# First modulation on TensorE, zero fills left out, first attention's stores from GpSimd, stick-breaking in float32 with sigmoids in PSUM

## The chip, the cores and the metric

The kernel runs on one core of a Trainium2 chip. The metric is the device time of one execution in microseconds (us). The kernel before takes 4246.98 us, the median of 3 runs (4244.62 to 4251.69).

## What is computed

Two blocks, one after the other, on 1024 tokens of width 1024, float32 throughout. The parts that the change touches:

```python
# first block: modulation of layer 0, for the tokens and for 256 context tokens
shift, scale, gate = split(silu(c) @ ada_w[0] + ada_b[0], 3)
shift_c, scale_c, gate_c = split(silu(c_ctx) @ ada_w[0] + ada_b[0], 3)
# layer 0: attention (8 heads over 2 kv heads, 8 heads over a latent), out = (o * silu(gate)) @ w_out
# layer 1: Hyena; its filters h = (hid @ w3 + b3) * decay are carried into the frequency domain
# second block, layer 0: causal convolution beside stick-breaking attention (8 heads of 64)
z = q @ k.T / 8;  log_1m = where(causal, log_sigmoid(-z), 0)
between = reverse_cumsum(log_1m) - log_1m
wts = where(causal, exp(log_sigmoid(z) + between), 0);  o = wts @ v
# layer 1: gated linear recurrence; after both layers a mixture of 16 experts
```

## The kernel before, in words

One program of 45506 instructions on five engines; a scheduler orders the instructions of each engine's queue by the dependences of tiles, so that loads may stand ahead of where the source has them. A queue is served strictly in its order. Matrix products are made from float32 operands split into a high and a low part of type float32r (`split`, L100 on ScalarE and L104 on VectorE), three matmuls each (`mm3`, L108 to L110).

**Spectra of the Hyena filters.** `hy_spectra` and `_filters` (L921 to L1070) make the filters in 8 chunks: `prepare` loads w3 and b3, splits them into `wa` and `wb` (rows 64 and 96 of `wb` carry the bias's high and low part, rows 65 to 95 are filled with zeros, L1005), four steps of matmuls with `wa` and `wb` (L1038, L1039) give PSUM tiles that VectorE multiplies by the decay (`fb`, L1041) and splits (`sd`). `_spectrum` turns a chunk into frequencies with 8 calls of `base`, 18 matmuls each at most; after three of every four calls it takes one step of the work in `self.aside`, and one step of `_filters` after each call.

**The first modulation** is that work aside: `mods` (L222) loads 16 row blocks of `ada_wT` (512 KB each, SP queue, ring of 3). Even blocks are multiplied and summed on VectorE, once for c and once for c_ctx (L236); odd ones are multiplied on GpSimd (L233) and summed on ScalarE (L234). silu(c) and silu(c_ctx) are made on rows of 1024 on all 128 partitions. It must be done before chunk 3.

**First attention.** `_a_project` (L338) projects the 1280 tokens; each result is normalised, rotated, split, and kept in DRAM by `store` (the high part's DMA from the ScalarE queue, the low part's from the GpSimd queue, L421), by `vstore` (L426) and by `gate` (L477), both from the ScalarE queue: 38 high parts, 38 low parts, 20 values, 16 gates. A loop over 38 projections takes one step of `beside` (22 products for latent keys and values, then 12 for latent queries) after each from the tenth on, the rest behind the loop. The keys' table `S["k"]` has 160 rows a head: high part, low part, a row of ones (L428), 31 rows of zeros that two SP DMAs write (L432). `a_load` reads the tables back for `_a_attend`, from the GpSimd queue.

**Stick-breaking attention.** `ev_attend` (L1565) goes over 32 units (head, group of 256 queries). Each has two rows of 128 queries: `scores` (L1608, L1611) gives z in PSUM (ring of 2 tiles of two banks), ScalarE writes sigmoid(-z) to SBUF (`e`, ring of 4), VectorE scans it backwards (L1620, with an operand of zeros from one column), GpSimd subtracts neighbours (`w`, L1624). `turn` transposes the weights on TensorE (L1636) and splits them into `th` and `tl`; `gather` (L1650) multiplies both by the values, which `values` (L1506 to L1508) has stored as high and low part side by side; the two halves of the sum are added by L1654 and L1656.

## Time and profile before

| | us |
|---|---|
| median of 3 runs | 4246.98 |
| the profiled execution, its own time | 4247.26 |
| its span, from the first to the last instruction | 4245.5 |
| PE busy / VectorE (DVE) busy / ScalarE (ACT) busy / GpSimd (POOL) busy | 3659.2 / 2932.2 / 1777.8 / 1031.8 |
| mean granted clock of TensorE | 0.931 of full speed |

A stage is read with the table by stretches: busy time of each engine, the granted clock of TensorE, and what the DMA engines moved. Which wait holds a stage is read from the timeline, where the brackets give the idle time ahead of an instruction and what ended it. PE is TensorE, and PEld its weight loads; SPq and ACTq are the DMA issues of the SP and ScalarE queues.

### The profile page before, as it was taken

Reading aid. Unit: us, or ns where it says so; the run is one execution under the profiler, and the core shown is the slowest. Engines: PE = TensorE matmul, PEld = TensorE weight load, DVE = VectorE, ACT = ScalarE, POOL = GpSimd, SP = SyncE. Lnnn points to the kernel's source line nnn. Section 1 sums busy time; section 2 is a strip of 40 time slices with the busy share of each in tenths; the row PEclk is TensorE's granted clock in tenths of the full one; section 3 lists DMA queues with packets and bytes.
Section 4 is the critical chain, followed back from the end, with each engine's and each line's share of the span. In section 5 each row is a group of like instructions: output and inputs, shape, how many; then the busy total and the mean of one; then the engine's idle time right before and its main releaser. Section 6 shows DMA issues by size and latency. Waiting matters only on the chain. (4 is left out here: it accounts for less than half of the span.)

```text
span 4245.5 us, 45506 instructions
## 1 busy us (share of the span) xinstructions
PE 3659.2 (86%) x16880; PEld 2817.5 (66%) x16880; DVE 2932.2 (69%) x3280; ACT 1777.8 (42%) x2458; POOL 1031.8 (24%) x628
## 2 busy tenths in 40 slices
PE   5799779999989999686989957879999788889997
PEld 4787564445568777675757746667887576667885
DVE  7996427787656774999667869565665777556664
ACT  4554334344343211111443345535655544546663
POOL 4740011111010012786000034321112134311112
PEclk9899898999999999887999979989999899989998
DMA  4553364534146882433322241347777310368786
GB/s 159 167 177 92 109 173 125 157 85 119 35 144 230 280 282 70 147 131 126 137 73 77 69 110 43 136 152 272 288 292 256 136 45 31 109 228 307 288 295 210
DMA packets 224278, 675.20 MB, mean 159 GB/s; under 512 B 54775, under 2 KB 79915, under 8 KB 188980
## 3 DMA queue, kind: packets, MB, share of 16 engines
q1 hardware_dynamic: 144806, 521.72, 35.4%
q0 software_dynamic: 61200, 107.01, 9.1%
q10 hardware_dynamic: 18046, 43.52, 2.9%
q8 instruction: 134, 2.20, 0.2%
q14 instruction: 92, 0.75, 0.1%
HBM read 538.04 MB, written 133.94 MB: 158 GB/s over the span
## 5 line engine op out<-in xcount | busy, mean ns | idle before, releaser
L104 DVE TENSOR_TENSOR wl<-wraw,wh 128x1024 fp32r<-128x1024 f32 (+1 forms) x214 | 332.1, 1561 | 266.8 <-ACT wh L100 253.4
L100 ACT CAST wh<-wraw 128x1024 fp32r<-128x1024 f32 (+1 forms) x214 | 277.4, 1308 | 487.9 <-PE pj L109 164.8
L108 PE MATMUL pj<-hh,wh 128*128 128x512 f32 x1024 | 408.2, 399 | 24.3 <-DVE u L1164 12.2
L110 PE MATMUL pj<-hh,wl 128*128 128x512 f32 x1024 | 403.1, 394 | 1.5 <-DVE wl L104 1.5
L109 PE MATMUL pj<-hl,wh 128*128 128x512 f32 x1024 | 403.9, 395 | 0.0
L108 PE MATMUL mm<-hh,wh 128*128 128x512 f32 (+3 forms) x832 | 338.0, 407 | 37.6 <-ACT wh L100 19.4
L110 PE MATMUL mm<-hh,wl 128*128 128x512 f32 (+3 forms) x832 | 329.5, 397 | 7.7 <-DVE wl L104 7.7
L109 PE MATMUL mm<-hl,wh 128*128 128x512 f32 (+3 forms) x832 | 331.6, 399 | 1.0 <-POOL hl L104 0.8
L123 ACT ACTIVATE pt<-st 128x512 f32<-128x512 f32 x320 | 181.7, 599 | 221.0 <-PE st L678 211.2
L108 PEld LDWEIGHTS pj<-hh,wh 128*128 128x128 f32 x1024 | 194.9, 190 | 74.8 <-issue 18.4
L661 DVE TENSOR_REDUCE mx<-s 128x1 f32<-128x1280 f32 x124 | 184.5, 1488 | 82.2 <-PE s L658 81.2
L110 PEld LDWEIGHTS pj<-hh,wl 128*128 128x128 f32 x1024 | 194.4, 190 | 44.4 <-DVE wl L104 2.3
L109 PEld LDWEIGHTS pj<-hl,wh 128*128 128x128 f32 x1024 | 194.6, 190 | 43.9 <-issue 3.4
L236 DVE SCALAR_TENSOR_TENSOR modw<-modw,c 128x1024 f32<-128x1024 f32 x128 | 160.6, 1268 | 83.3 <-DMA modw<-in_mod_wT_dram 60.4
L108 PEld LDWEIGHTS mm<-hh,wh 128*128 128x128 f32 (+1 forms) x832 | 160.1, 193 | 86.0 <-issue 18.1
L104 DVE TENSOR_TENSOR l<-raw,h 128x1024 fp32r<-128x1024 f32 x128 | 165.2, 1322 | 66.0 <-ACT h L100 64.3
L684 PE MATMUL ps_o<-pt,v 128*64 128x512 f32 x640 | 209.8, 615 | 0.7 <-ACT pt L123 0.4
L1321 PE MATMUL py<-c_g,ph 128*128 128x256 f32 x512 | 135.8, 426 | 79.7 <-DVE ph L1200 79.7
L110 PEld LDWEIGHTS mm<-hh,wl 128*128 128x128 f32 (+1 forms) x832 | 159.6, 192 | 46.4 <-DVE wl L104 10.2
L109 PEld LDWEIGHTS mm<-hl,wh 128*128 128x128 f32 (+1 forms) x832 | 160.1, 192 | 39.5 <-DVE hl L877 1.9
L2199 POOL DMA_INDIRECT xg<-m_h,idx x50 | 62.4, 1247 | 467.8 <-PE xt L2113 421.2
L1321 PEld LDWEIGHTS py<-c_g,ph 128*128 128x128 f32 x512 | 107.4, 215 | 102.5 <-issue 67.2
(602 smaller groups left out, 9840.8 us busy)
## 6 DMA issues: line engine op xcount, KB each, us to landing
wraw<-in_ex_w_dram SPq DMA_DIRECT2D x128, 1024.0 KB
raw<-in_ex_w_dram SPq DMA_DIRECT2D x64, 1024.0 KB
modw<-in_mod_wT_dram SPq DMA_DIRECT2D x96, 512.0 KB
modw<-in_ada_wT_dram SPq DMA_DIRECT2D x48, 512.0 KB
m_y<-ys ACTq DMA_DIRECT2D x48, 512.0 KB
ks<-kt SPq DMA_DIRECT2D x64, 256.0 KB
wraw<-in_w_hy_in_dram SPq DMA_DIRECT2D x16, 1024.0 KB
kk<-ks SPq DMA_DIRECT2D x28, 512.0 KB
```

Of the source, the lines that this page charges most:

```text
L100: nc.scalar.copy(hi, src)
L104: e.tensor_tensor(out=lo, in0=src, in1=hi.bitcast(F32), op=ALU.subtract)
L108: nc.tensor.matmul(ps, wh, xh, start=first, stop=False)
L109: nc.tensor.matmul(ps, wh, xl, start=False, stop=False)
L110: nc.tensor.matmul(ps, wl, xh, start=False, stop=last)
L123: ins = act.activation(out, in_, func, **kw).ins
L236: nc.vector.scalar_tensor_tensor(out=junk, in0=w, scalar=1.0, in1=c, op0=ALU.mult, op1=ALU.mult, accum_out=o[:, j:j + 1])
L661: nc.vector.tensor_reduce(out=mx[:, j:j + 1], in_=s[:, :TK] if own else m3, op=ALU.max, axis=AX.X, negate=True)
L684: nc.tensor.matmul(ps_o[e * 64:(e + 1) * 64], st[2 * hp + e]["v"][:, kb], pt[:, e], start=kb == 0, stop=kb == NK - 1)
L1321: nc.tensor.matmul(py[:, j], d["ph"][:, r, cs], g[:, m, r], start=k == 0, stop=k == 3)
L2199: self.nc.gpsimd.indirect_dma_start(out=out, out_offset=None, in_=src, in_offset=bass.IndirectOffsetOnAxis(ap=ix, axis=0))
```

## The change

The first modulation becomes `first_mods`: the untransposed weights (8 loads of 1 MB, SP queue, ring of 2) are the moving operand of 32 float32 matmuls, 4 to a load, each with 32 columns (of which two carry silu(c) and silu(c_ctx)) and its own 32 output partitions; a copy, four transposes and two copies bring the result into columns. The spectra's PSUM ring gives up one of six banks for it. The bias rows of the filters are split once for all chunks and put into `wb` by two GpSimd DMAs a chunk, its zero rows are filled once. `S["k"]` loses its 31 zero rows, and what is read of it is 65 rows in place of 96. All stores of the first attention's projections are issued by GpSimd, and `beside` begins four projections later. The stick-breaking attention keeps the values and the weights whole in float32, works on both heads of a pair at once (64 output partitions each), takes rows in another order, and writes the sigmoid over z in PSUM, from where VectorE scans it.

```diff
...
+    def first_mods(self, pool, pp, outs):
...
+        nc = self.nc
+        sc = pool.tile([P, 8, 32], F32, name="mc")
+        nc.vector.memset(sc, 0.0)
+        self.act(sc[:, :, 0:2], self.vec("cond", 0, 16).rearrange("p (k c) -> p k c", c=2), AF.Silu)
+        yield
+        ps = pp.tile([P, 512], F32, name="md", tag="md")
+        ws = []
+        for k in range(9):
+            if k < 8:
+                w = pool.tile([P, 2048], F32, name="modw", tag="modw", bufs=2)
+                nc.sync.dma_start(w, self.a["ada_w0"][k * P:(k + 1) * P])
+                ws.append(w)
+            if k:
+                for q in range(4):
+                    nc.tensor.matmul(ps[32 * q:32 * q + 32], sc[:, k - 1], ws[k - 1][:, q * 512:(q + 1) * 512],
+                                     start=k == 1, stop=k == 8)
+            yield
+        t = pool.tile([P, 512], F32, name="mt")
+        nc.scalar.copy(t, ps)
+        yield
+        pt = pp.tile([P, 4, P], F32, name="md", tag="md")
+        for b in range(4):
+            nc.tensor.transpose(pt[:, b], t[:, b * P:(b + 1) * P], self.ident)
+        yield
+        for i, o in enumerate(outs):
+            nc.vector.tensor_copy(o[:, 0:16].rearrange("p (q b) -> p b q", b=4), pt[:, :, i::32])
+        yield
...
-            for name, shape in (("q", [8, 2, 64, T]), ("k", [2, 160, TK]), ("v", [P, 10, P]),
+            for name, shape in (("q", [8, 2, 64, T]), ("k", [2, 129, TK]), ("v", [P, 10, P]),
...
-                    (nc.gpsimd if i else nc.scalar).dma_start(ap_of(dst, i * off * pitch + t0, dims), src.bitcast(F32))
+                    nc.gpsimd.dma_start(ap_of(dst, i * off * pitch + t0, dims), src.bitcast(F32))
...
-                nc.scalar.dma_start(dst[:, b], t)
-            nc.sync.dma_start(ap_of(S["k"], 128 * TK, [[P, 10], [160 * TK, 2], [1, P]]),
+                nc.gpsimd.dma_start(dst[:, b], t)
+            nc.sync.dma_start(ap_of(S["k"], 128 * TK, [[P, 10], [129 * TK, 2], [1, P]]),
                               ap_of(self.ones1, 0, [[self.ones1.ap[0][0], 10], [0, 2], [1, P]]))
-            zero = self.blk64[0:31, 64:128]
-            for i in range(2):
-                nc.sync.dma_start(S["k"][i, 129:160].rearrange("r (b t) -> r b t", t=64),
-                                  ap_of(zero, 0, [zero.ap[0], [0, TK // 64], [1, 64]]))
...
-                nc.scalar.dma_start(S["gate"][m, :, pt[0]:pt[0] + 512], g)
+                nc.gpsimd.dma_start(S["gate"][m, :, pt[0]:pt[0] + 512], g)
...
-                if n >= 10:
+                if n >= 14:
...
-                kb = kp.tile([96, 1, TK], F32R, name="kb", tag="kb")
+                kb = kp.tile([65, 1, TK], F32R, name="kb", tag="kb")
...
-            nc.gpsimd.dma_start(qb[:, :, :n], qs[0:96, :, :n])
+            nc.gpsimd.dma_start(qb[0:64, :, :n], qs[0:64, :, :n])
...
-        with tc.tile_pool(name="sp_c", bufs=1) as cp, tc.tile_pool(name="sp_ps", bufs=6, space=PSUM) as pp, \
+        with tc.tile_pool(name="sp_c", bufs=1) as cp, tc.tile_pool(name="sp_ps", bufs=5, space=PSUM) as pp, \
...
+        b3 = wp.tile([8, 2, 256], F32, name="b3", tag="w3", bufs=1)
+        for o in range(2):
+            nc.sync.dma_start(b3[4 * o:4 * o + 4], ap_of(a["hy_b3"], 2 * o * D, [[256, 4], [D, 2], [1, 256]]))
+        bs = wp.tile([8, 2, 256], F32, name="bs", bufs=1)
+        bh, bl = [wp.tile([8, 2, 256], F32R, name="b" + q, bufs=1) for q in "hl"]
+        for d, op in ((0, ALU.add), (1, ALU.subtract)):
+            nc.vector.tensor_tensor(out=bs[:, d], in0=b3[:, 0], in1=b3[:, 1], op=op)
+        self.split(bh, bl, bs)
+        wbs = [wp.tile([97, 2, 256], F32R, name=f"wb{i}", bufs=1) for i in range(2)]
+        for t in wbs:
+            nc.vector.tensor_copy(t[64:96].rearrange("p a b -> p (a b)"), self.zero_row(512)[64:96])
...
-            b3 = wp.tile([97, 2, 256], F32, name="b3", tag="b3", bufs=1)
             nc.sync.dma_start(w3, a["hy_w3"].rearrange("k (o d c) -> k o d c", o=2, d=2)[:, o, :, cs])
-            nc.sync.dma_start(b3[64:97], ap_of(a["hy_b3"], o * 2 * D + ch * 256, [[0, 33], [D, 2], [1, 256]]))
...
                 nc.gpsimd.tensor_tensor(out=ws[:, d], in0=w3[:, 0], in1=w3[:, 1], op=op)
-                nc.gpsimd.tensor_tensor(out=bs[64:97, d], in0=b3[64:97, 0], in1=b3[64:97, 1], op=op)
             wa = wp.tile([P, 2, 256], F32R, name="wa", tag="wa", bufs=2)
-            wb = wp.tile([97, 2, 256], F32R, name="wb", tag="wb", bufs=2)
-            b3h = wp.tile([97, 2, 256], F32R, name="b3h", tag="b3h", bufs=1)[96:97]
+            wb = wbs[(o * 4 + ch) % 2]
             nc.scalar.copy(wa, ws)
             nc.vector.tensor_tensor(out=wb[0:64], in0=ws[0:64], in1=wa[0:64].bitcast(F32), op=ALU.subtract)
-            nc.vector.tensor_copy(wb[64:96].rearrange("p a b -> p (a b)"), self.zero_row(512)[64:96])
-            nc.scalar.copy(wb[64:65], bs[64:65])
-            nc.scalar.copy(b3h, bs[96:97])
-            nc.vector.tensor_tensor(out=wb[96:97], in0=bs[96:97], in1=b3h.bitcast(F32), op=ALU.subtract)
+            for r, t in ((64, bh), (96, bl)):
+                nc.gpsimd.dma_start(wb[r:r + 1], t[o * 4 + ch:o * 4 + ch + 1])
...
-                t = tp.tile([P, 4, 2, 64], F32R, name="vhl", tag="vhl")
-                src = ps.rearrange("p (h e) -> p h e", e=64)
-                nc.scalar.copy(t[:, :, 0], src)
-                nc.vector.tensor_tensor(out=t[:, :, 1], in0=src, in1=t[:, :, 0].bitcast(F32), op=ALU.subtract)
-                nc.sync.dma_start(S["ev"][4 * c:4 * c + 4, :, b, :].rearrange("h p e -> p h e"),
-                                  t.rearrange("p h a e -> p h (a e)").bitcast(F32))
+                t = tp.tile([P, 256], F32, name="vs", tag="vhl")
+                nc.scalar.copy(t, ps)
+                nc.sync.dma_start(S["ev"][:, b, c * 256:(c + 1) * 256], t)
...
+                q, k = [ip.tile([P, 2, 2 * T if n == "k" else T], F32R, name=n, tag=n) for n in "qk"]
+                v = ip.tile([P, 8, P], F32, name="v", tag="v")
...
-                nc.gpsimd.dma_start(v, S["ev"][2 * hp:2 * hp + 2].rearrange("h p b e -> p h (b e)"))
+                nc.gpsimd.dma_start(v, S["ev"][:, :, hp * P:(hp + 1) * P])
...
-                e = wp.tile([P, T], F32, name="e", tag="e", bufs=4)[:, :n]
-                self.act(e, z[:, :n], AF.Sigmoid, scale=-1.0)
+                e = z[:, :n]
+                self.act(e, e, AF.Sigmoid, scale=-1.0)
...
-                w = wp.tile([P, T], F32, name="w", tag="w", bufs=6)[:, :n]
+                w = wp.tile([P, T], F32, name="w", tag="w", bufs=8)[:, :n]
...
-                th = wp.tile([P, 2, 256], F32R, name="th", tag="th", bufs=5)
-                tl = wp.tile([P, 2, 256], F32R, name="tl", tag="tl", bufs=5)
+                t = wp.tile([P, 2, 256], F32, name="wt", tag="wt", bufs=8)
...
-                    self.split(th[:, 0], tl[:, 0], pt[:, 0].rearrange("p j q -> p (j q)"))
-                    self.split(th[:, 1, P:], tl[:, 1, P:], pt[:, 1, 1])
...
                 else:
-                    self.split(th, tl, pt.rearrange("p b j q -> p b (j q)"))
...
+                    nc.scalar.copy(t, pt.rearrange("p b j q -> p b (j q)"))
+                return t
+            def gather(hp, g, ps_o, c, ts):
+                last = c == g
                 for b in range(2):
                     q0 = P if last and b == 1 else 0
-                    for x, t in enumerate((th, tl)):
-                        nc.tensor.matmul(ps_o[:, q0:], st[h]["v"][:, c + b], t[:, b, q0:],
-                                         start=c == 0 and b == 0 and x == 0, stop=last and b == 1 and x == 1)
+                    for e in range(2):
+                        nc.tensor.matmul(ps_o[e * 64:e * 64 + 64, q0:], st[2 * hp + e]["v"][:, 2 * c + b],
+                                         ts[e][:, b, q0:], start=c == 0 and b == 0, stop=last and b == 1)
                 if last:
-                    tmp = wp.tile([P, 256], F32, name="tmpo", tag="tmpo")
-                    nc.scalar.copy(tmp[64:128], ps_o[64:128])
-                    r = h % 2 * 64
-                    nc.vector.tensor_tensor(out=o[r:r + 64, 4 + h // 2, g * 256:(g + 1) * 256], in0=tmp[64:128],
-                                            in1=ps_o[0:64], op=ALU.add)
+                    nc.scalar.copy(o[:, 4 + hp, g * 256:(g + 1) * 256], ps_o)
...
-            todo = [(2 * hp + e, 3 - i if e == 0 else i) for hp in range(4) for i in range(4) for e in range(2)]
+            todo = [(hp, g) for hp in range(4) for g in (3, 0, 2, 1)]
+            rows = [(2 * hp + e, 2 * g + j) for hp, g in todo for j in range(2) for e in range(2)]
             es, ws, pend = {}, {}, []
-            for i in range(-2, len(todo)):
-                if i >= 0 and i % 8 == 2 and i < 24:
-                    load(i // 8 + 1)
-                if i >= 0:
-                    h, g = todo[i]
+            for r in range(-6, 4 * len(todo)):
+                i, t = r // 4, r % 4
+                if i >= 0 and i % 4 == 0 and t == 3 and i < 12:
+                    load(i // 4 + 1)
+                if 0 <= r + 4 < len(rows):
+                    ws[r + 4] = weights(*es.pop(r + 4))
+                if r + 6 < len(rows):
+                    es[r + 6] = scores(*rows[r + 6])
+                if i < 0:
+                    continue
+                hp, g = todo[i]
+                if t == 0:
                     ps_o = pp.tile([P, 256], F32, name="po", tag="po")
-                for t in range(4):
-                    if t < 2 and 0 <= i + 1 < len(todo):
-                        ws.setdefault(i + 1, []).append(weights(*es[i + 1][t]))
-                    if t < 2 and i + 2 < len(todo):
-                        q = todo[i + 2]
-                        es.setdefault(i + 2, []).append(scores(q[0], 2 * q[1] + t))
-                    if i >= 0 and t <= g:
-                        pend.append((h, g, ps_o) + turn(ws[i], 2 * g + 2, 2 * t))
-                    if len(pend) > 2:
-                        gather(*pend.pop(0))
+                if t <= g:
+                    pend.append((hp, g, ps_o, t, [turn([ws[4 * i + e], ws[4 * i + 2 + e]], 2 * g + 2, 2 * t)
+                                                  for e in range(2)]))
+                if len(pend) > 2:
+                    gather(*pend.pop(0))
...
-            self.aside = self.mods(mp, a["ada_wT"][0], ("c", "c_ctx"), (m["l0"], m["c0"]), 0, 16, 3, 2)
+            mpp = tc.alloc_tile_pool(name="mod_ps", bufs=1, space=PSUM)
+            self.aside = self.first_mods(mp, mpp, (m["l0"], m["c0"]))
+            self.step()
...
```

## Rows read from the trace of the kernel before

**Rows 1.** Table by stretches: stretch, us, busy and instructions by engine, granted clock, DMA share, GB/s.

```profile
52.00:304.00 252.00, 206.02 (x1468) 197.39 (x1468) 238.86 (x337) 138.38 (x252) 151.91 (x105) 0.91 0.47 154
208.00:220.00 12.00, 12.00 (x99) 11.83 (x98) 10.31 (x19) 7.36 (x15) 5.02 (x5) 1.00 0.42 142
415.00:525.00 110.00, 83.86 (x306) 61.70 (x305) 44.73 (x68) 41.55 (x58) 11.61 (x15) 0.84 0.38 108
525.00:606.00 81.00, 81.00 (x360) 61.47 (x359) 27.98 (x43) 28.63 (x46) 7.38 (x10) 1.00 0.61 164
2466.00:2663.00 197.00, 139.13 (x864) 122.86 (x864) 172.94 (x215) 101.17 (x215) 89.24 (x74) 0.88 0.24 60
```

**Rows 2.** Timeline, 13 to 53 us: start, us, instruction, [idle before, what ended it].

```profile
13.54 17.58 SPq L432 DMA_DIRECT2D s_k<-blk  x2
...
30.38 0.58 PE L1039 MATMUL pf<-wb,hb 97*128 97x256 f32 x1 [1.26 <-DVE wb L1008]
...
46.61 2.34 POOL L233 TENSOR_TENSOR modj<-modw,c 128x1024 f32<-128x1024 f32 x1 [28.57 <-DMA modw<-in_ada_wT_dram]
...
50.17 2.29 DVE L236 SCALAR_TENSOR_TENSOR modj<-modw,c 128x1024 f32<-128x1024 f32 x1 [19.84 <-ACT modj L234]
...
52.39 1.28 DVE L1041 TENSOR_TENSOR fb<-pf,dec 128x512 f32<-128x512 f32 x2
```

**Rows 3.** VectorE's groups, 50 to 304 us: count, busy us, mean ns, idle before.

```profile
L104 DVE TENSOR_TENSOR sd<-fb,sd 128x512 fp32r<-128x512 f32 x64 | 63.0, 1003 | 3.0 <-ACT sd L100 2.9
L1041 DVE TENSOR_TENSOR fb<-pf,dec 128x512 f32<-128x512 f32 x64 | 41.2, 676 | 0.0
L236 DVE SCALAR_TENSOR_TENSOR modw<-modw,c_ctx 128x1024 f32<-128x1024 f32 x7 | 21.7, 3096 | 0.0
...
L236 DVE SCALAR_TENSOR_TENSOR modj<-modw,c 128x1024 f32<-128x1024 f32 x7 | 9.6, 1365 | 19.8 <-ACT modj L234 19.8
...
L1008 DVE TENSOR_TENSOR wb<-bs,b3h 1x512 fp32r<-1x512 f32 x7 | 8.1, 1153 | 0.2
...
L1005 DVE CAST wb<-zero_col 32x512 fp32r<-32x512 f32 x6 | 5.5, 916 | 0.1
```

**Rows 4.** Stores of line 421, 397 to 570 us: ns min/median/max, first and last start.

```profile
L421 ACTq DMA_DIRECT2D s_km<-sth x15: 325/2179/9411, 397.8 to 568.2; - x15
L421 POOL DMA_DIRECT2D s_km<-stl x15: 586/796/798, 398.8 to 570.0; - x15
```

**Rows 5.** Waits, 415 to 525 us: who waited for whom, us, times, longest.

```profile
PE mm L297 <- ACT sqa L287: 21.4, 4, 7.0
```

**Rows 6.** Timeline from the end of the projections to the first scores.

```profile
617.80 11.90 ACTq L421 DMA_DIRECT2D s_qm<-sth  x2
...
638.35 1.44 PE L658 MATMUL s<-ka,qa 128*128 128x512 f32 x3 [23.06 <-ACT wk L544]
```

**Rows 7.** Groups by line, stick-breaking, 2466 to 2662 us.

```profile
L1620 DVE TENSOR_TENSOR_SCAN c<-e,zero_col 128x896 f32<-128x896 f32 (+3 forms) x64 | 109.5, 1724 | 14.1 <-ACT e L123 13.6
L1608 PE MATMUL z<-k,q 128*128 128x512 f32 (+2 forms) x192 | 55.2, 404 | 32.0 <-issue 29.3 <-ACT e L123 2.7
L104 DVE TENSOR_TENSOR tl<-pt,th 128x512 fp32r<-128x512 f32 (+2 forms) x112 | 52.9, 485 | 7.9 <-ACT th L100 7.0
...
L1636 PE MATMUL pt<-ident,w 128*128 128x128 f32 x288 | 52.1, 305 | 52.9 <-DVE tl L104 50.7 <-POOL w L1624 1.6
...
L123 ACT ACTIVATE e<-z 128x896 f32<-128x896 f32 (+3 forms) x64 | 41.8, 656 | 22.0 <-PE z L1611 17.4 <-DVE c L1620 2.5 <-PE pt L1636 1.7
...
L1656 DVE TENSOR_TENSOR o<-tmpo,po 64x256 f32<-64x256 f32 x31 | 12.9, 416 | 1.0
```

**Rows 8.** Timeline of VectorE: one scan of a row of 896 keys.

```profile
2646.94 2.03 DVE L1620 TENSOR_TENSOR_SCAN c<-e,zero_col 128x896 f32<-128x896 f32 x1 [0.45 <-ACT e L123]
```

**Rows 9.** Timeline of TensorE: runs of float32 matmuls, 64 and 128 output partitions.

```profile
908.96 2.79 PE L684 MATMUL ps_o<-pt,v 128*64 128x512 f32 x10
...
2400.57 1.89 PE L1464 MATMUL side<-u,dg 128*128 128x512 f32 x4
```

More of the change, by code (lines that the diff above doesn't have):

```diff
@@ L51 @@
 for _n, _c in [("norm_w0", 8), ("norm_w1", 8), ("ada_b0", 24), ("ada_b1", 24), ("q_norm", 1), ("k_norm", 1),
-               ("cq_norm", 2), ("ckv_norm", 1), ("final_w", 8),
+               ("cq_norm", 2), ("ckv_norm", 1), ("final_w", 8), ("cond", 16),
                ("mod_b0", 48), ("mod_b1", 48), ("mix_g0", 8), ("mix_g1", 8), ("ffn_g0", 8), ("ffn_g1", 8),
@@ L449, in key @@
                     rope(kk, pt, swap16)
-                store(kk, S["k"], 64, 160, 2, 64, TK, pt)
+                store(kk, S["k"], 64, 129, 2, 64, TK, pt)
             def query_latent(pt, pss):
@@ L610, in a_load @@
                 nc.gpsimd.dma_start(qa[:, :, n:], qs[:, :, n:])
-                nc.gpsimd.dma_start(qb[:, :, n:], qs[0:96, :, n:])
+                nc.gpsimd.dma_start(qb[0:64, :, n:], qs[0:64, :, n:])
         return qa, qb, ka, kb, v
@@ L643, in load @@
                         d["guess"] = (qa[:, e], ka[:, 0])
-                        d["mm"] = [(qa[:, e], ka[:, 0]), (qb[:, e], kb[:, 0])]
+                        d["mm"] = [(qa[:, e], ka[:, 0]), (qb[0:65, e], kb[:, 0])]
                         d["row"] = qb[64:65, e]
@@ L1585, in load @@
             def load(hp):
-                q, k, v = [ip.tile([P, 2, 2 * T if n == "k" else T], F32R, name=n, tag=n) for n in "qkv"]
+                q, k = [ip.tile([P, 2, 2 * T if n == "k" else T], F32R, name=n, tag=n) for n in "qk"]
+                v = ip.tile([P, 8, P], F32, name="v", tag="v")
                 if hp:
@@ L1644, in turn @@
-                return c, last, th, tl
-            def gather(h, g, ps_o, c, last, th, tl):
+                    nc.scalar.copy(t[:, 0], pt[:, 0].rearrange("p j q -> p (j q)"))
+                    nc.scalar.copy(t[:, 1, P:], pt[:, 1, 1])
+                else:
+                    nc.scalar.copy(t, pt.rearrange("p b j q -> p b (j q)"))
+                return t
+            def gather(hp, g, ps_o, c, ts):
+                last = c == g
                 for b in range(2):
                     q0 = P if last and b == 1 else 0
-                    for x, t in enumerate((th, tl)):
-                        nc.tensor.matmul(ps_o[:, q0:], st[h]["v"][:, c + b], t[:, b, q0:],
-                                         start=c == 0 and b == 0 and x == 0, stop=last and b == 1 and x == 1)
+                    for e in range(2):
+                        nc.tensor.matmul(ps_o[e * 64:e * 64 + 64, q0:], st[2 * hp + e]["v"][:, 2 * c + b],
+                                         ts[e][:, b, q0:], start=c == 0 and b == 0, stop=last and b == 1)
@@ L2280, in program @@
             S = {"eq": dr.tile([8, P, T], F32, name="eq"), "ek": dr.tile([8, P, T], F32, name="ek"),
-                 "ev": dr.tile([8, P, 8, P], F32, name="ev")}
+                 "ev": dr.tile([P, 8, 512], F32, name="ev")}
             M = self.moe_dram(dr)
@@ L2302, in program @@
             self.hy_spectra(ks, invn, early)
+            mpp.release()
             o, o_pool = self.phase_a(first, m["l01"], M)
@@ L2456, in layout @@
     o["ident"] = np.eye(P, dtype=np.float32)
+    o["ada_w0"] = np.ascontiguousarray(g["ada_w"][0][:, :2048])
     o["c_2"] = np.ascontiguousarray(g["c_2"][0])
@@ L2470, in layout @@
         put(f"ffn_g{l}", g["ffn_norm_g_2"][l])
+    put("cond", np.stack([g["c"][0].reshape(-1), np.asarray(g["c_ctx"]).reshape(-1)], axis=1).reshape(8, P, 2)
+        .transpose(0, 2, 1).reshape(-1))
     put("q_norm", np.tile(g["attn_q_norm"][0], 2))
```

7 lines of the change are left out of this document (3 added, 4 removed).

## The prediction

> **What bounds the kernel now.** I began with the page: TensorE is busy for 86% of the span, so work taken from another engine only counts where TensorE is not the limit. The table by stretches shows which places these are [rows 1]. In 52 to 304 us (spectra, with the modulation beside them) VectorE works 238.86 of 252 us and TensorE 206.02. In 415 to 525 us no engine is full: 306 matmuls take 110 us at a granted clock of 0.84, and right behind 360 of the same kind take 81 us at 1.00. In 2466 to 2663 us (stick-breaking) VectorE works 172.94 of 197 us, TensorE 139.13. The stages that lie between are touched only in their operands, and I forecast nothing there. For each of the three I then read which wait ends last, in timeline, groups and waits.
>
> The sum is made against the profiled execution, 4247.26 us, which is 0.3 us above the median. A measurement of this kernel tells a difference from none above some 0.2%, 8.5 us.
>
> **Start.** TensorE has its first filter product at 30.38 us, but VectorE multiplies it by the decay at 52.39 [rows 2]. The reason stands in the brackets: VectorE's `modj` waits for ScalarE, which waits for GpSimd, whose 28.57 us of idle time end with a `modw` load; and the SP queue that issues it was held by the zero fill of `s_k` from 13.54 to 31.1. Both links go. With the product at 30.38 the first `fb` can start at about 31; what is late next is the new `b3`, which shares w3's buffer, so that the first w3 load, and the SP queue behind it, waits for VectorE's two adds. Two DMAs for the first `wb` lie in that chain as well. Bounds 0 (that chain is as late) and 27; I take **22**.
>
> **Spectra.** From VectorE go the modulation's products (21.7 + 9.6, of which the 2.29 of the first is counted above, and 1.0 of accumulator reads: 30), the zero fills 5.5 and the bias subtractions 8.1 [rows 3]. `sd` has the shape of `fb`, yet takes 1003 ns against 676: 64 × 0.327 = 21 us of lengthening while GpSimd, which loses 16 products of 2.34 us [rows 2], and others work; I give half back, 10. Added are about 2 us of copies. 238.9 − 30 − 13.6 − 10 + 2 = 187. TensorE does 99 matmuls in 12.00 us when nothing holds it [rows 1], so its 1468 need 178. The new 32 float32 matmuls have 512 columns; four such take 1.89 us [rows 9], 0.47 each, 15 in all, 193 together. The stretch lies 13 us above its busiest engine now; with two engines this close and one PSUM bank fewer I put it 19 above: 212, so **40**. Bounds: each of the eight 1 MB loads is waited for in full, 8.4 MB at the 154 GB/s of this stretch, 54 us, which leaves nothing; and 64 if VectorE's 187 alone counts. The two small DMAs a chunk go to GpSimd, which loses 16 products and 16 bias operations; 16 × 0.8 us [rows 4] are covered by its 252 − 152 us idle. The second half of the wb ring is the cover of their landing; without it each chunk would wait for a landing.
>
> **Projections.** A high part's store holds ScalarE's queue for 325 to 9411 ns, 2179 at the median, where the low part's, issued by GpSimd, takes 586 to 798 [rows 4]. Behind it in ScalarE's queue stand squares and splits, and TensorE waits for these: 21.4 us in four waits for `sqa` [rows 5]. At the later stretch's 81/360 = 0.225 us a matmul the 306 would take 69 of the 110 us, so 41 is the most; I take **25**, since VectorE's splits stay and the lower clock may come from the loads. GpSimd gets 74 stores more, 112 in all; at 0.8 us these are 90 us in the 302 us from 304 to 606, beside 19 us of work in 191 us [rows 1]. A store that waits for its operand now holds those behind it on one queue, and the `sth` buffers come free later for it. Bounds 0 and 41.
>
> **End of the projections.** TensorE stands idle for 23.06 us ahead of the first scores, while two `s_qm` stores hold ScalarE's queue for 11.90 us [rows 6]. That goes, but `beside` starts four projections later, so that 10 of its 34 products are left behind the loop where 6 were; and the loads of the tables stand in GpSimd's queue behind the last stores. Four products more take about 24 × 0.225 = 5 us each if nothing is beside them, 20, less what fills the idle time. Bounds −15 and +20; I take **8**. The 31 rows fewer that are read are costed at nothing: SP and GpSimd have idle time here, and the number of columns of each matmul is the same.
>
> **Stick-breaking.** VectorE loses the subtractions `tl`, 52.9, and the additions `o`, 12.9 [rows 7]. The 64 scans take 109.5, 1724 ns each; one alone, 896 keys, took 2.03 us [rows 8], 2.27 ns an element, so that 64 of 576 keys on average need 84 undisturbed. A scan that reads PSUM is nowhere in the trace; its price is bounded by these two, 84 and 110 (reading no faster than SBUF). TensorE loses 320 float32r matmuls of 256 columns at 0.121 (38 us) for 160 float32 ones of 64 columns; ten of 512 take 2.79 [rows 9], 0.14 for 256 columns, 22 in all: 139 − 38 + 22, about 121. ScalarE's copies stay at its 101 us [rows 1].
>
> So the ring of two z tiles decides, since z is now held through sigmoid and scan: scores 55.2/64 = 0.86, sigmoid 0.656, scan 1.31 to 1.71 (84 and 110 over 64) [rows 7], and, as an estimate, 0.2 to 0.6 for the handovers between the three engines; 3.0 to 3.8 a row with two rows in flight, 97 to 122 us for 64. The scores of row r + 6 wait on TensorE for the scan of r + 4, and behind them in its queue stand the transposes and gathers of row r, for which ScalarE and GpSimd's next steps wait. To this come filling, draining and waits: 24 us now (197 − 173), 14 at the least (the idle time ahead of scans). 111 to 146; I take 132, not far above the middle, **gain 65**. The bounds of the whole stage: without any overlap 64 × 3.8 = 242, a loss of 46; and 110, ScalarE's busy time with some filling, a gain of 87.
>
> Sum: 22 + 40 + 25 + 8 + 65 = 160; 4247 − 160 = **4087**.
>
> **The rule against it.** Four float32 matmuls of 512 columns take 1.89 us, 0.47 each [rows 9], twice the 0.225 of the projections [rows 1]. The Trainium skill, page FP8 and Floating Point Precision, section TensorE Precision Notes, says that true FP32 takes four passes through the array; by that a matmul would take four times the single one, not twice, and the trace does not agree. By the rule the time is that of rival C, 4156 in place of 4087.
>
> **Rivals.**
> A. *The z ring holds the stage.* TensorE's queue is in order, so a late scan delays transposes, these delay the copies, and the handovers add up. At 165 to 195 us the stage gains 2 to 32, here 20: 4132. For it: VectorE's sigmoid wait is already the largest idle time ahead of scans, 13.6 us [rows 7]. Against it: two rows stay in flight. Chance 0.18.
> B. *Spectra stay held*, by TensorE with one bank fewer or by loads of 1 MB that come late on SP. Gain there 5: 4122. For it: TensorE's 193 is above VectorE's 187. Chance 0.12, with A together (4167) 0.04 more.
> C. *Float32 runs at four passes.* Gathers 160 × 0.45 = 72 in place of 22, with TensorE then at 171 and the stage at 186: 55 lost; modulation 32 × 0.90 = 29 in place of 15: 14. 4156. Against it: rows 9 have the same kinds of matmul, at half of that. Chance 0.03.
> D. *The slow store belongs to its destination, not to ScalarE's queue* (slower). If all 74 moved stores take 9.41 us on GpSimd, 696 + 30 for the low parts, in a stage of 302 us: 424 longer, less the other gains of 127, 4544. It decides from a mean of (302 + 127 − 30)/74 = 5.4 us. Against it: the low parts of the same shape never exceed 0.80 [rows 4]. Chance 0.03.
> E. *The change does nothing in its largest place*, because stick-breaking and spectra both gain under 10 us: 4175. Chance 0.02.
>
> **Numbers.** The forecast's own case has 0.58. 4035 is the sum of better ends that can come together (27, 55, 35, 10, 85); 4170 takes in A, B, both together and C. Faster 0.95, within 0.2% 0.02, slower 0.03.
>
> **What would show it.** First `fb` near 31 us (start); no modulation product on VectorE and 304 us become some 240 (spectra); GpSimd's stores near 0.8 us, and no wait of TensorE for `sqa` between 415 and 525 (projections); a stick-breaking stage of 132 us with scans of 1.3 to 1.7 us, gathers 0.14 apart and TensorE's waits ended by VectorE's scans. I am wrong if the stage stays above 165, if GpSimd's stores take over 2 us, or if matmuls in spectra wait for `modw`.

## The result, and the profile after

The changed kernel takes 4151.17 us (median of 4 runs, 4145.65 to 4161.05), the kernel before, measured with it, 4248.95. The ratio is 0.9774, interval 0.9757 to 0.9790: 98 us less, where 160 were forecast. The profiled execution took 4151.53 us, its span 4149.8.

The span is cut at landmarks that both kernels have: the first decay product (`fb`), the last `kt` of the spectra, the first and last scores `s` of the first attention, the first `z` and the last output `o` of the stick-breaking attention. The table gives lengths in us, worked out from the first and last starts of these instructions (of the last output, its end) in each kernel's one profile.

| kernel | to first fb | spectra | to first s | attention | to first z | stick-breaking | rest |
|---|---|---|---|---|---|---|---|
| before | 52.4 | 251.1 | 334.9 | 520.4 | 1307.8 | 196.1 | 1582.8 |
| changed | 40.1 | 224.3 | 326.0 | 523.1 | 1295.4 | 153.1 | 1587.8 |
| forecast of the change | -22 | -40 | -33 | 0 | 0 | -65 | 0 |
| found | -12 | -27 | -9 | +3 | -12 | -43 | +5 |

Three columns that the change hardly touches vary from run to run: the fourth between 517 and 530, the fifth between 1295 and 1309, the last between 1580 and 1594 over the profiles below (without experiment 10's). So the -12 of the fifth column is not read as a gain, and stick-breaking took 148 us, not 153, in all later runs of this same code. The third column varies too: from 317.5 to 330.3 over the changed kernel and the eight later profiles with the same code there, and by 10 over the two with the code before (334.9, and 345.0 in experiment 5). So its -9 is one draw of a gain between 4 and 28.

The table by stretches of the changed kernel, columns as in [rows 1], for spectra, projections and stick-breaking:

```profile
40.10:264.40 224.30, 201.65 (x1491) 187.41 (x1490) 191.32 (x298) 111.31 (x206) 103.27 (x87) 0.95 0.50 163
376.00:486.00 110.00, 96.61 (x392) 74.28 (x391) 50.73 (x79) 45.68 (x63) 32.32 (x42) 0.94 0.56 129
486.00:560.00 74.00, 70.61 (x315) 52.75 (x313) 22.17 (x33) 27.01 (x45) 23.15 (x37) 1.00 0.71 187
2408.90:2562.00 153.10, 131.66 (x864) 95.59 (x864) 87.61 (x69) 90.93 (x198) 80.90 (x74) 0.93 0.24 64
```

VectorE has lost what was forecast (191 against 187 in the spectra, 88 in stick-breaking). TensorE is now the fuller engine in both, with 202 where 193 was forecast and 132 where 121 was. The spectra have 23 us of TensorE's idle time, the projections' first stretch 392 matmul records in 110 us where it had 306.

The timeline of the start shows why the first `fb` came at 40 and not at 31:

```profile
22.04 1.88 PE L257 MATMUL md<-modw,mc 128*32 128x512 f32 x2 [9.93 <-DMA modw<-in_ada_w_dram]
23.85 3.78 PE L980 MATMUL pf<-hid,w 64*128 64x512 f32 x4
...
40.15 1.29 DVE L1073 TENSOR_TENSOR fb<-pf,dec 128x512 f32<-128x512 f32 x2 [5.02 <-PE pf L1071]
```

TensorE stood for 9.93 us at the first modulation matmul until its load had landed, and the second product of the filters' hidden layer stood behind that. In all its waits for `modw` take 14.0 us ahead of the first `fb`, and 2.0 behind it.

The waits of the spectra have a new one that was small before (here the row of before, then the changed kernel's; us in total, times, longest):

```profile
PE pf L1015 <- DVE absacc L1012: 2.8, 4, 1.0
```

```profile
PE pf L1047 <- DVE absacc L1044: 17.3, 8, 3.7
```

This is a one-column matmul for a chunk's norm, eight times, that waits for VectorE's sum.

Stores of the projections (ns min/median/max, first and last start), then the end of the projections on TensorE and the buffers' waits of ScalarE and VectorE ahead of it:

```profile
L452 POOL DMA_DIRECT2D s_km<-sth x15: 601/798/807, 386.8 to 512.6; - x15
L452 POOL DMA_DIRECT2D s_qm<-sth x12: 691/798/850, 538.0 to 601.2; - x12
```

```profile
PE mm L328 <- ACT sqa L318: 10.0, 2, 9.4
```

```profile
564.89 0.62 ACT L100 CAST sth<-wk 128x512 fp32r<-128x512 f32 x1 [6.95 <-DMA s_qm<-sth]
...
584.75 0.69 DVE L104 TENSOR_TENSOR stl<-wk,sth 128x512 fp32r<-128x512 f32 x1 [14.78 <-DMA s_qm<-stl]
...
590.36 1.44 PE L685 MATMUL s<-ka,qa 128*128 128x512 f32 x3 [33.02 <-ACT wk L571]
```

No store takes over 0.88 us, against 9.41 in [rows 4], and TensorE waits 10.0 us for `sqa` where it waited 21.4 [rows 5]. But the idle time ahead of the first scores has grown from 23.06 [rows 6] to 33.02.

Groups of the stick-breaking stage, columns as in [rows 7]:

```profile
L1650 DVE TENSOR_TENSOR_SCAN c<-z,zero_col 128x896 f32<-128x896 f32 (+7 forms) x64 | 85.1, 1352 | 58.9 <-ACT z L123 57.7 <-ACT wt L1670 1.1
L1654 POOL TENSOR_TENSOR w<-c 128x896 f32<-128x896 f32 (+7 forms) x64 | 72.6, 1146 | 89.9 <-DVE c L1650 76.9 <-PE pt L1666 12.9
L1638 PE MATMUL z<-k,q 128*128 128x512 f32 (+3 forms) x192 | 55.8, 408 | 43.3 <-issue 27.9 <-DVE c L1650 11.4 <-DMA k<-ek 3.6
L1666 PE MATMUL pt<-ident,w 128*128 128x128 f32 x288 | 45.1, 287 | 5.5 <-POOL w L1654 5.5
...
L1681 PE MATMUL po<-wt,v 128*64 128x256 f32 (+1 forms) x320 | 40.8, 370 | 0.0
```

Scans fell from 1724 to 1352 ns, the short end of the bounds (84 us). VectorE now waits 57.7 us for the sigmoid where it waited 13.6. TensorE waits for scans, whose end frees a z tile, for 11.4 us only; it is busy for 132 of the 153.

### The profile page after: what moved, and what is told of

It is laid out like the page before. It is cut to its first block, busy times and chain, and to the rows that moved or that the text cites. A ratio compares the mean times of both kernels' runs of the same rounds, so it can differ in the third digit from the quotient of the medians.

```text
span 4149.8 us, 45164 instructions
## 1 busy us (share of the span) xinstructions
PE 3649.7 (88%) x16948; PEld 2778.2 (67%) x16948; DVE 2788.9 (67%) x3080; ACT 1739.7 (42%) x2395; POOL 1024.4 (25%) x686
## 5 line engine op out<-in xcount | busy, mean ns | idle before, releaser
L108 PE MATMUL mm<-hh,wh 128*128 128x512 f32 (+3 forms) x832 | 335.0, 404 | 35.9 <-ACT wh L100 18.9
L109 PEld LDWEIGHTS pj<-hl,wh 128*128 128x128 f32 x1024 | 194.9, 190 | 44.3 <-issue 3.4
```

The costliest lines, as they stand in the source:

```text
L108: nc.tensor.matmul(ps, wh, xh, start=first, stop=False)
L109: nc.tensor.matmul(ps, wh, xl, start=False, stop=False)
```

## The experiments

Every kernel but the fifth starts from the changed kernel; diffs show only what differs. Stages are those of the table above, and 4151 is the changed kernel's median.

**1. The modulation behind the first filter products.**

```diff
-                    nc.tensor.matmul(ps[32 * q:32 * q + 32], sc[:, k - 1], ws[k - 1][:, q * 512:(q + 1) * 512],
-                                     start=k == 1, stop=k == 8)
+                    self.behind(nc.tensor.matmul(ps[32 * q:32 * q + 32], sc[:, k - 1], ws[k - 1][:, q * 512:(q + 1) * 512],
+                                                 start=k == 1, stop=k == 8).ins, [self.last_pf])
...
```

(`last_pf` is the last filter matmul of chunk 0's first step; `behind` keeps the order of two instructions of one engine.)

> The changed kernel with one thing more: the modulation's float32 matmuls must stand behind the first four filter products in TensorE's queue. Theory: in the changed kernel the hidden layer's second product stands behind a modulation matmul that waited 9.93 us for its load, and that is what put the first decay product (fb) at 40.15 us. Expected: hidden layer's second product near 15 us in place of 23.85, first fb at 30 to 33 us, the last kt at 254 to 258 in place of 264.4, total 7 to 10 us below the changed kernel's 4151. Rival: the first fb is set by the w3 load and by ScalarE's copies, which the order of TensorE doesn't touch; then fb stays at 38 to 40 and the total within 3 us.

```profile
15.34 3.86 PE L980 MATMUL pf<-hid,w 64*128 64x512 f32 x4 [2.87 <-ACT hid L123]
...
30.49 1.33 DVE L1075 TENSOR_TENSOR fb<-pf,dec 128x512 f32<-128x512 f32 x2 [3.54 <-PE pf L1071]
```

These two rows of its timeline are the theory's: 15.34 and 30.49 us. The last `kt` came at 257.3 in place of 264.4. The order in TensorE's queue, not the w3 load, held the start: in the four profiles with this edit (experiments 1, 9, 11, 12) the first `fb` comes between 30.3 and 30.7 us, in the others of the changed kernel never before 39.8. The median is 4144.13 us, 7 below (0.9754, 0.9732 to 0.9775); that interval overlaps the changed kernel's, so the gain in the total is not clear of noise.

Two more rows of this run show what the modulation's matmuls cost at a granted clock of 1.00: four of them (eight records, see below), each on its own 32 output partitions, take no longer than one alone.

```profile
34.29 1.06 PE L257 MATMUL md<-modw,mc 128*32 128x512 f32 x8
...
41.02 1.05 PE L257 MATMUL md<-modw,mc 128*32 128x512 f32 x2
```

**2. The work beside from the tenth projection again.** (`if n >= 14` to `if n >= 10`.)

> The changed kernel with the work beside starting at the tenth projection again, so that 6 products are left behind the loop and not 10. Theory: the ten left over set TensorE's idle time of 33.0 us ahead of the first scores, because each waits for a buffer of a store that takes 14.6 us to land. Expected: idle 20 to 25 us, total 8 to 12 below 4151. Rival: the idle time is set by the table loads in GpSimd's queue; then it stays at 30 or more, and the four products more only lengthen the loop: total within 4 us of 4151.

The stretch from last `kt` to first scores fell from 326.0 to 315.1, TensorE's idle time ahead of the scores to 17.3 us:

```profile
PE s L685 <- ACT wk L571: 17.3, 1, 17.3
```

The total is 4151.31 (0.9776, 0.9755 to 0.9796): the same. The attention behind took 528.6 in place of 523.1; its first 29.6 us had 49 matmul records where the changed kernel has 58 in the same time. Both expectations hold in part. The late start does cost the idle time, which is 29.6 to 36.1 us in every other profile with it and with the stores on GpSimd. An earlier first score brings nothing in the total; but 530 us of attention were also seen with the late start (experiment 1), and 317.5 to the first scores (experiment 10), so neither the giving back nor the size of the gain in the stage is shown by this one run.

**3. The sigmoid in SBUF again.**

```diff
-                e = z[:, :n]
-                self.act(e, e, AF.Sigmoid, scale=-1.0)
+                e = wp.tile([P, T], F32, name="e", tag="e", bufs=4)[:, :n]
+                self.act(e, z[:, :n], AF.Sigmoid, scale=-1.0)
```

> The changed kernel with the sigmoid written to SBUF again (four buffers), all the rest of the new stick-breaking kept. Theory: the ring of two z tiles, held through sigmoid and scan, holds the stage at 153 us (first scores to last output). With z free after the sigmoid VectorE's idle time for ScalarE falls from 57.7 to under 25 us and the stage to 125 to 138, total 15 to 28 below 4151, if the scan stays near 1.35 us. Rival: the scan is short because it reads PSUM; from SBUF it takes 1.7 us again (109 us in all) and the stage stays at 145 to 160, total within 8 us of 4151.

It went the rival's way and further: 4186.79 us (0.9858, 0.9838 to 0.9878), 36 slower, the stage 178.2 us. The groups:

```profile
L1650 DVE TENSOR_TENSOR_SCAN c<-e,zero_col 128x896 f32<-128x896 f32 (+7 forms) x64 | 124.3, 1985 | 44.3 <-ACT e L123 43.9 <-POOL w L1654 0.4
L1654 POOL TENSOR_TENSOR w<-c 128x896 f32<-128x896 f32 (+7 forms) x64 | 105.5, 1669 | 81.7 <-DVE c L1650 55.2 <-PE pt L1666 24.4 <-PE z L1641 2.0
L1666 PE MATMUL pt<-ident,w 128*128 128x128 f32 x288 | 48.4, 302 | 35.6 <-POOL w L1654 35.4 <-ACT wt L1672 0.2
```

Both sides of an overlap are longer, VectorE's scan (1985 against 1352 ns) and GpSimd's subtraction (1669 against 1146), and TensorE now waits 35.4 us for the subtraction.

**4. The 74 stores on ScalarE again.** (`nc.gpsimd.dma_start` to `nc.scalar.dma_start` for high parts, values and gates; the late start kept.)

> The changed kernel with the 74 stores (high parts, values, gates) issued by ScalarE again, the later start of the work beside kept. Theory: the stores held ScalarE's queue and thereby TensorE; from the last kt to the last product of the loop it takes 293 us in the changed kernel and will take 306 to 315; total 10 to 20 above 4151. Rival: the time in the stage came from the later start of the work beside, the loads or the granted clock; then the stage stays at 290 to 298 and the total within 5 us.

4200.16 us (0.9898, 0.9873 to 0.9922): 49 slower, more than either expectation. From last `kt` to first scores it takes 374.5 us, 46.8 of them the idle time of TensorE at the end; without this it is 327.7 against 293.0, where 306 to 315 were expected. Two rows, the stores of line 452 and the timeline of ScalarE's queue:

```profile
L452 ACTq DMA_DIRECT2D s_qm<-sth x12: 500/1043/20309, 572.5 to 649.1; - x12
```

```profile
582.25 20.31 ACTq L452 DMA_DIRECT2D s_qm<-sth  x1
602.67 1.09 ACT L571 ACTIVATE wk<-mm 128x512 f32<-128x512 f32 x2 [20.46 <-issue]
```

One store held ScalarE for 20.31 us. Together with experiment 2 this bounds what the move of the stores is worth: 374.5 - 326.0 = 49 us at the late start, and at the early one 334.9 - 315.1 = 20, there with the other edits of this stage and one run each.

**5. Five banks in the kernel before.** (`sp_ps` from 6 to 5, nothing else.)

> The kernel before with five PSUM banks for the spectra in place of six, nothing else changed. Theory: the bank that the modulation takes costs part of the gain that the spectra lack (27 of the 40 us forecast); from the first fb to the last kt, 251 us before, it takes 255 to 262. Rival: the bank is not missed, the stage stays at 249 to 253 and the total within 3 us of before.

The spectra took 250.7 us against 251.1. The total was 1.0014 of before (1.0000 to 1.0027), with the 10 us more in the projections, where nothing was changed. The bank is not missed by the kernel before; whether the changed one, where VectorE is no longer the bound, would miss it was not tried.

**6. Three z tiles,** and one tile each for `pt` and `po` in place of two.

> The changed kernel with three z tiles, and one tile each for the transposed weights and the output in place of two. Theory A, the z ring holds the stick-breaking stage: it falls from 148 to 153 us (first scores to last output, as measured) to 125 to 138. Theory B, TensorE's own work of 132 us with the handovers of its in-order queue holds it: 143 to 150. Theory C, the transposes' tile becomes the wait in its place: over 155.

Theory C: the stage took 159.1 us, the total 4165.02 (0.9800, 0.9779 to 0.9822). ScalarE's copies show the new wait:

```profile
L1672 ACT COPY wt<-pt 128x512 f32<-128x512 f32 x48 | 28.1, 586 | 29.1 <-PE pt L1666 28.9
```

It was 7.2 us in the changed kernel. On A against B this run says nothing, since its third z tile was paid for with the second `pt`.

**7. Half of the gathering.** (`for b in range(2)` to `range(1)`.)

> The changed kernel with every second key block left out of the gathering of the values (80 float32 matmuls of 160), so that its output lacks these blocks. No z tile, scan or copy is touched. Theory B, TensorE's busy time holds the stage: that falls from 132 by 15 to 20 us, and the stage from 148 to 130 to 138. Theory A, the ring of z tiles with scores, sigmoid and scan in turn holds it: the stage stays at 144 to 150 though TensorE has less to do.

TensorE's busy time fell by 10 us, the stage by 3 from the 148 of the other runs; the total is 4146.60 us. The row of the stage, then TensorE's waits for scans, here and in experiment 2, whose stage took 148.3:

```profile
2415.80:2560.80 145.00, 122.12 (x704) 86.35 (x704) 87.64 (x69) 90.75 (x198) 80.90 (x74) 0.91 0.24 67
```

```profile
PE z L1638 <- DVE c L1650: 12.8, 15, 4.1
```

```profile
PE z L1638 <- DVE c L1650: 9.7, 13, 3.4
```

The stage stays in A's range, and B alone, which would give 138 for 10 us less, does not fit. But less was taken from TensorE than expected (15 to 20), and A is not shown by it: TensorE is busy for 132 of the 148 us (122 of 145 here), and of its 16 us of idle time (23 here) the wait for scans is 10 (13). The rest of what it no longer works went to waits for a load of k (3.1 in place of 0.5 us) and for the subtraction (6.0 in place of 5.3). So, as far as these rows go, TensorE's own work and the turn around two z tiles hold the stage together; how much the ring alone costs is open.

**8. One block of the modulation.** (Loop to 1 of 8 blocks.)

> The changed kernel with one of the eight row blocks of the first modulation: 7 loads of 1 MB and 28 of 32 float32 matmuls are left out, so its modulation is incomplete. It bounds what the modulation on TensorE still costs. Theory: the early loads and matmuls delay the hidden layer (10 us, as the second experiment of this study showed at 30.5 us) and take TensorE's time later; first fb at 30 to 33 and first fb to last kt 208 to 216 in place of 224, total 15 to 25 below 4151. Rival: the rest of the stage doesn't feel them: 222 to 226 from first fb to last kt, total 5 to 10 below.

(The expectation says second experiment where it means the first.) A miss for the total: 4159.16 us, more than with all blocks. The first `fb` came later, at 44.3: the statistics of the attention's input, which need the modulation done, moved to the front, and eight loads of `xt` and squares on ScalarE stood ahead of the copies for `wb`. From first `fb` to last `kt` it took 215.6, 9 less than with all eight blocks, the theory's end of the range. As the statistics moved too, this is no clean price of the modulation. Nor could the first `fb` come at 30: the one block that is left still stands ahead of the hidden layer's second product, which starts at 24.19 us.

**9. The norm's matmul one step later,** with experiment 1 kept.

```diff
...
                 if c == 0 and last:
                     total(*last)
+                if c == 1 and last:
+                    total2(*last)
...
```

(`total` keeps VectorE's sum; `total2` has the two matmuls, the reciprocals and GpSimd's scaling. `absacc` has two buffers; `bs` shares the buffer of `ws`.)

> The changed kernel with the modulation behind the first filter products (as in e1_mods_behind) and with the two one-column matmuls of a chunk's norm (and GpSimd's scaling of the skip row behind them) emitted one step later, VectorE's sum before them where it was; the sum's buffer is doubled for it. Theory: with VectorE's load gone, TensorE's new wait in the spectra is the norm's matmul for that sum, 17.3 us in eight waits in the changed kernel, 2.8 in the kernel before; moved, it falls under 6 us, and first fb to last kt from 226.8 (e1_mods_behind) to 208 to 217, total 8 to 18 below e1's 4144. Rival: the wait passes to another product of the same queue (for fb or sd); then 222 to 228 and the total within 5 us of 4144.

```profile
PE pf L1049 <- DVE absacc L1044: 5.1, 1, 5.1
PE pf L1049 <- DVE fb L1077: 4.6, 4, 2.3
```

The wait fell from 18.9 (experiment 1) to 5.1 us, and 4.6 passed to `fb`. The spectra took 220.1 us against 226.8, two thirds of the least that was expected; the total is 4135.31 (0.9734, 0.9721 to 0.9747), 9 below experiment 1, though the two intervals overlap. (The spectra took 221.0 and 221.5 us in experiments 12 and 11, which keep this edit, and 222.3 to 226.8 in all others of the changed kernel with the whole modulation.)

**10. No subtraction,** with the sigmoid in SBUF as in experiment 3.

```diff
...
-                w = wp.tile([P, T], F32, name="w", tag="w", bufs=8)[:, :n]
-                nc.gpsimd.tensor_tensor(out=w, in0=rev(n - 1), in1=rev(n), op=ALU.subtract)
-                return w
+                return c[:, 1:n + 1]
...
```

> e3_e_in_sbuf (sigmoid in SBUF) with GpSimd's 64 subtractions left out: the transposes read the scan's output itself, so the output is not that of stick-breaking, and GpSimd is idle in the stage. Theory: a scan that reads and writes SBUF is lengthened while GpSimd works; without that work all scans take what they take from PSUM, 1.30 to 1.40 us on average (1.98 in e3), and the stage falls from 178 to 140 or less. Rival: SBUF as the source is slow in itself; then the mean stays at 1.8 to 2.0.

```profile
L1650 DVE TENSOR_TENSOR_SCAN c<-e,zero_col 128x896 f32<-128x896 f32 (+7 forms) x64 | 83.6, 1347 | 37.6 <-ACT e L123 37.6
```

The time from PSUM within 5 ns: 1347. The stage took 131.1 us, with TensorE busy for 123.8 of them at a granted clock of 0.97, where it was 132 at 0.92 in experiment 2. (The ring of the scan's outputs has 10 places in place of 5 here, as the transposes read it. The whole took 5305.45 us, with 2762.8 for the layers behind alone, which get other values; only the stage is read.)

**11. A small third z tile,** of one bank, for every second row of up to 512 keys, on top of experiment 9; `po` has one tile for it.

> e9_total_later with one z tile more, of one bank, for every second row of up to 512 keys (the output's tile goes from two to one for it). Theory: as the ring of z tiles holds the stick-breaking stage, a third place for a quarter of the rows takes 4 to 9 us from its 148. Rival: the single output tile makes the gathers wait for ScalarE's copy, 16 times 0.4 us and handovers, and the stage is the same or longer, 147 to 156.

The stage took 150.2 us, the total 4139.87 (0.9736, 0.9720 to 0.9752): no gain, in the rival's range. Whether the third place would help with both output tiles kept is open.

**12. Two table loads behind the last stores,** on top of experiment 9: `qa` and `qb` of the second 512 queries are issued after the loop over what is left of `beside`.

> e9_total_later with two of the first attention's table loads (the second 512 queries, qa and qb) issued after the last projections' stores in place of ahead of them. Theory: in TensorE's idle time ahead of the first scores (33.0 us in the changed kernel) a table load stands in GpSimd's queue for about 10 us until an earlier one has landed, and the stores behind it free their buffers that much later; with it gone the idle time falls to 20 to 26 us and last kt to first scores from 322.3 (e9_total_later) to 310 to 316; total 4 to 10 below e9's 4135 if the attention doesn't give it back. Rival: the buffers wait for the landing of the stores themselves (14.6 us median), whatever stands between them; then idle time stays at 30 or more and the total within 4 us of 4135. A second one: the idle time falls, and the attention (525.8 us from first to last scores in e9_total_later) is longer by as much, as with the work beside from the tenth projection on.

The waits of TensorE, first of experiment 9, then of this kernel:

```profile
PE s L685 <- ACT wk L571: 32.0, 1, 32.0
```

```profile
PE s L686 <- DMA s_qm<-sth: 29.6, 1, 29.6
```

The load that had stood 10.58 us in GpSimd's queue is gone, but only 2.4 us of the idle time with it. That is nearest to the first rival: what ends the wait is now a store's landing itself (12.9 us at the median here, 14.6 in the changed kernel). 4134.34 us (0.9731, 0.9714 to 0.9749) is not distinct from experiment 9.

Experiments 9, 11 and 12, which all keep the edits of experiment 9, are below the changed kernel, their intervals apart from its own.

## Why the prediction was right, and where its terms were not

The direction and the range held (4035 to 4170); the sum was 62 to 64 us too large, and four terms carry that. The forecast's own case, with 0.58, did not come. The range held because it took in the rivals: 4151 lies between A (4132) and A with B (4167), and parts of both are what the runs show. Of the three signs of being wrong one came: matmuls waited for `modw`, though nearly all of that ahead of the first `fb`.

**Start, 22 forecast, 12 found.** The mechanism was right: both links went, and the b3 chain was early (its adds ended near 12.3 us). The term failed at its "TensorE has its first filter product at 30.38": it took that order of TensorE's queue from the kernel before. The 32 new matmuls were costed as time of TensorE, not as instructions that wait for loads ahead of others. Experiment 1 puts the hidden layer first and finds 22, as forecast.

**Spectra, 40 forecast, 27 found.** VectorE's working was right within 4 us. The step that failed is TensorE's 193: it has 202, which is 9 of the 12 us that are missing against 212, while the margin above it is 23 where 19 was taken. Two rows of the stretch, of experiment 1 with all 32 modulation matmuls in it and of experiment 8 with none, say which part of the 193 was short:

```profile
30.50:257.30 226.80, 206.97 (x1522) 188.74 (x1522) 191.13 (x297) 110.94 (x206) 103.54 (x87) 0.95 0.53 173
```

```profile
44.30:259.90 215.60, 193.32 (x1452) 187.40 (x1453) 187.56 (x284) 107.30 (x199) 104.78 (x87) 0.96 0.45 144
```

The modulation's 15 came out, at 14, but by luck: one such matmul takes twice the 0.47 us of the forecast (below), and four run in the time of one. The filters' 178 are 193. They were priced by 12 us of [rows 1] at a granted clock of 1.00, while the whole stretch had 0.91 before and has 0.95 now; that the clock is all of the difference is not shown. Of the margin, 17 us are the wait for the norm's sum, off the path when VectorE was the bound. Experiment 9 takes 14 us from that wait (18.9 to 5.1) and 7 from the stage. The PSUM bank that I named for this margin costs the kernel before nothing (experiment 5).

**Projections and their end, 33 forecast, 9 found.** Without the idle time at its end the stage fell from 311.8 to 293.0 us, 19 of the 25 forecast for the stores, though one run each and a stage that varied by 10 between experiment 5 and before; that the stores' place carries it is shown by experiment 4. The error is in the end: 8 us of gain were taken where the rows gave -15 to +20, and 10 of loss came (23.06 to 33.02 us of idle time). The four products more find four buffers each of `sth` and `stl` whose stores take 14.6 us to land; a wait for a landing came where ScalarE's wait for the issue had been. Experiment 12 shows that the loads between them are little of it.

**Stick-breaking, 65 forecast, 43 found (48 in the later runs).** The step that failed is "So the ring of two z tiles decides", with TensorE's 121 us inside it. TensorE is busy for 132 us, as long as the whole stage was forecast, and the 16 us that it is idle in the later runs come on top; 10 of them are waits for scans, rival A's mechanism, which had a chance of 0.18 for a gain of 2 to 32. Experiment 7 shows that neither TensorE's sum nor the ring holds the stage alone. That the working of the ring (3.0 to 3.8 us for the turn of one tile) was wrong is not shown, since at 2.3 us a row TensorE's own work takes 2.1. With the tile free after the sigmoid, scans of the same length and no subtraction (experiment 10) the stage takes 131, and TensorE is busy for 124 of it.

Two prices in this term were read wrongly. The first is the float32 matmul. In the program 160 gathers are issued, in the trace stand 320; and before, 320 instructions of L684 stand as 640. The 32 modulation matmuls leave 64, and the four that are left in experiment 8 leave 8. Each float32 matmul leaves two records, so the ten and the four of [rows 9] were five and two matmuls, and 0.47 us was the price of half of one. The whole takes 1.89/2 = 0.95 us, 4.2 times the 0.225 of a float32r one. The Trainium skill, page FP8 and Floating Point Precision, section TensorE Precision Notes (four passes), was therefore right, and my sentence that the trace does not agree was wrong. Rival C's sum still did not come, since matmuls with few output partitions run side by side on their own columns, as the two rows of experiment 1 show for four of 32. For the two heads of the gathers, in a run of 24 records, 12 matmuls,

```profile
2559.18 2.38 PE L1681 MATMUL po<-wt,v 128*64 128x256 f32 x24
```

take 2.38 us, 0.20 each where 0.14 was forecast and rival C had 0.45. For 160 that would be 10 us more, as much as TensorE's 132 against 121; but the 80 that experiment 7 leaves out, 32 of them with 128 columns, took 10 us with them, 0.12 each, so where the 11 us come from is open.

The second is the scan from PSUM, bounded by 84 and 110 and found at 85. Writing the sigmoid over z looked like a risk (z is held longer) and is worth 30 us of the stage net (178.2 against 148), 36 of the total. A scan of two SBUF operands and GpSimd's subtraction lengthen each other: the scan takes 1985 ns beside it, but 1352 with one operand in PSUM and 1347 with GpSimd idle; the subtraction takes 1669 beside the one scan and 1146 beside the one from PSUM. The Trainium skill, page SBUF — State Buffer, section SBUF: two separate sides, says it beforehand: VectorE and GpSimd share a pair of ports, which a VectorE instruction with two SBUF inputs holds against a GpSimd one that reads SBUF. These three runs agree: scan and subtraction are longer only where a scan with two SBUF operands runs beside the subtraction.

The slower side, rival D, fell with the first view: no store on GpSimd took over 0.88 us. The slowness belongs to ScalarE's queue: it came back with it (20.31 us in experiment 4).

## What to carry to other kernels

Work that moves to an idle-looking engine also moves its waits there: ask what stands behind each new instruction in that engine's queue and when its load lands, not only how long it takes. When the fullest engine of a stage is relieved, look at every small wait of the next one for it, and order those instructions anew. Count instructions in the program beside records in the trace before a row becomes a price, and look at the granted clock of the row that gives it: 12 us at 1.00 here made 178 of what took 193.

## What the runs showed of the hardware that was not expected

A float32 matmul stands in the trace as two records (160 and 320, 32 and 64). Four float32 matmuls of 512 columns, each with its own 32 output partitions, take 1.06 us, one alone 1.05. A DMA issue can hold ScalarE's queue for 20.31 us, while GpSimd's issues of the same shape take 0.85 at most. The same scan takes 1352 ns from PSUM, 1985 from SBUF beside GpSimd's subtraction, and 1347 from SBUF with GpSimd idle.
